# A hybrid decoder block on one core: transposed x as a second input, values of the first head group from raw x, the norm's row factor applied afterwards, and the first keys ahead of the first queries

## The chip, the cores and the metric

The kernel runs on one core of one Trainium2 chip. The metric is the device time of one execution in microseconds (us). A core has five engines that run side by side and meet at semaphores: TensorE (PE in the profile; its weight loads are PEld), VectorE (DVE), ScalarE (ACT), GpSimd (POOL) and SyncE (SP), which issues most of the DMAs. Each engine works through its own queue in the order in which the program stands.

## The reference

One sequence of 512 tokens of 1024 channels gets 16 meta tokens in front. The block normalises each row, multiplies it by one wide matrix and splits the result in eight parts; only the first four matter here:

```python
def rmsnorm(x, w):
    xf = x.astype(jnp.float32)
    y = xf * lax.rsqrt(jnp.mean(xf * xf, axis=-1, keepdims=True) + NORM_EPS)
    return (y * w.astype(jnp.float32)).astype(x.dtype)
...
u = rmsnorm(h, mix_norm_w[l])
proj = u @ w_in[l]
q, k, v, g_ret, lru_in, lru_gate, gate_a, gate_b = jnp.split(proj, split_at, axis=-1)
q = rotary(q.reshape(B, T, RET_HEADS, RET_QK_DIM).astype(f32), pos)
k = rotary(k.reshape(B, T, RET_HEADS, RET_QK_DIM).astype(f32), pos) * (RET_QK_DIM ** -0.5)
v = v.reshape(B, T, RET_HEADS, RET_V_DIM).astype(f32)
o = chunk_retention(q, k, v)
```

Behind it come a gated linear recurrence, gates that merge the two branches, an output projection and a feed-forward block with a second and a third rmsnorm. All is float32.

The norm has two factors: one per channel (the weight w) and one per row (the reciprocal root of the mean square). For a value row v = (x * w * r) @ W the row factor r can be applied to x before the product or to the finished row after it.

## The kernel before, in words

**Numbers.** A float32 operand is split into two parts, hi (a cast to the type that TensorE reads at full speed) and lo (the rest), and a product is made of three: hi by hi, hi by lo, lo by hi. So each quarter of a weight (128x512, called raw_...) costs one cast on ScalarE (line 290) and one subtraction on VectorE (line 294), and some go through POOL.

**Layout of x.** The 512 rows are four tiles of 128 tokens. TensorE needs the normed x with channels on the partitions. Before, x is loaded by rows (x_sb). For each tile ScalarE takes the sum of squares (Square with a sum, line 484), POOL makes the row factor and multiplies the identity by it (lines 476 to 490: a diagonal), and TensorE multiplies x by that diagonal (line 523, the uT tiles), which transposes and scales in one step; `halve` does half a tile, four blocks of 128 channels. Then `store` multiplies by the channel weight (line 508), casts (511) and subtracts (513). The result lies in four blocks, b11 and b21 (the lower and upper 512 channels of tokens 0 to 255), b12 and b22 (the same of tokens 256 to 511). Eight meta columns stand behind each of them, so a block is 264 columns wide, and 4 x 264 = 1056 in all.

**Fast and plain slabs.** A weight slab of 256 columns is either plain (four quarters; `plain512`, and for the keys 528 columns, `plain`) or fast: seven products instead of eight, with weight sums s1 to s4 on POOL (line 260) and four differences of x blocks, t1 to t4 (`sums_of`, lines 532 to 536: a subtraction, a cast and a subtraction each, on VectorE and ScalarE). The first queries Q0 are fast; the first keys K0, the first gates G0 and the values of the first head group are plain.

**The first stage.** The order of the first 45 us is written by hand in `FIRST_STEPS`: F is a row factor, T a transposition, x, h, l are the three steps of `store`, H and L the cast and the subtraction of the next weight quarter (P: the subtraction on POOL), W warm products, v the next step of `plain_values`. `plain_values` takes the eight quarters w_v for tile 0, tile 1, then both with the second four, then tiles 2 and 3; its accumulators are evicted by ScalarE (line 753). The meta rows get a path of their own (`norm_meta`, lines 567 to 585). Inside `manual_schedule` the engines keep the written order; behind it a planner orders each engine's queue. Then `ret_project` makes Q0, K0, G0, then the same for the other heads. Work that can be late (`defer`, `tick`) is put between products as their estimated time passes; `sums_of` for x is such an item, and in the first group it runs beside the last value products.

**Loads.** `FIRST_LOADS` is the order of the first DMAs on SyncE's queue: w0 to w3 are weight quarters of the values, x1 to x3 tiles, m the meta rows. Weight quarters have eight buffers (RAW), their hi and lo parts nine (RING).

Of the kernel before, what the change touches and what calls it, by code (L numbers as in the profile page):

```python
# [153 lines left out]
def hybrid_block(ctx: ExitStack, tc: tile.TileContext, a: dict):  # L154
# [16 lines left out]
    x_sb = [get(D) for t in range(NC_)]  # L171
    m_sb = get(D)
    nc.sync.dma_start(x_sb[0], a["x"][:C, :])
# [368 lines left out]
    UF, U, UFV, UV = blocks_of(TH)  # L542
    for load in FIRST_LOADS.split():
        if load[0] == "w":
            key, i, c = pieces[int(load[1:])]
            quarter(key, i, {"a11": 2, "a12": 3}[c])
        elif load == "m":
            nc.sync.dma_start(m_sb[:NM], a["meta"])
        else:
            t = int(load[1:])  # L550
            nc.sync.dma_start(x_sb[t], a["x"][t * C:(t + 1) * C, :])

    diags, halves = {}, {}

    def halve(t, c):

        pb = transposed(x_sb[t], diags[t], c, f"uT{t}_{c}")
        o = (t % 2) * C
        halves[t, c] = store(UFV, UV, pb, c, t // 2, slice(o, o + C), vec[:, V_MIX + 4 * c:V_MIX + 4 * c + 4])
        if c == 0:  # L560
            put(x_sb[t], diags.pop(t))
# [5 lines left out]
    def norm_meta():  # L567
        xn = get(D)
        nc.scalar.activation(xn[:NM], m_sb[:NM], AF.Copy, scale=diags.pop("m"))
        pm = bank("pm")  # L570
        for k in range(KT):
            nc.tensor.transpose(pm[:, k * NM:(k + 1) * NM], xn[:NM, k * P:(k + 1) * P], ident[:NM, :NM])
# [5 lines left out]
        nc.vector.tensor_tensor(um[:, :KT], pm, w, op=ALU.mult)
# [139 lines left out]
    def plain_values():  # L718

        acc = {}  # L720
        ws = {}
# [24 lines left out]
        pm = bank("vm0")
        for n, name in enumerate(PLAIN_V):
            _, h, c = name
            half, k = int(c[1]) - 1, int(c[2]) - 1
            value_meta(pm[:, half * 256:half * 256 + 256], ws[name], 4 * k + 2 * h, n == 0)  # L750
        vt = [get(D) for tok in range(2)]
        for t in range(NC_):
            nc.scalar.copy(vt[t // 2][:, t % 2 * 512:(t % 2 + 1) * 512], acc[t])
        vm = small.tile([2 * NM, 512], F32, tag="vm", bufs=2, name="vm0")
        nc.scalar.copy(vm, pm[:2 * NM])
# [4 lines left out]
    def first_steps(v):  # L760
        lows, meta = [], norm_meta()
        for step in FIRST_STEPS:
# [6 lines left out]
            elif kind in "LP":  # L769
                lows.pop(0)(nc.vector if kind == "L" else nc.gpsimd)  # L770
            elif kind == "W":
                keep_warm(WARM_MORE)
            elif step == "Fm":
                diags["m"] = rms_factors(m_sb[:NM], "m", NM, False)
            elif step in ("Tm", "xm"):
                next(meta, None)
            elif kind == "F":
                diags[int(t)] = rms_factors(x_sb[int(t)], f"x{t}")
            elif kind == "T":
                halve(int(t), int(c))  # L780
            elif kind in "xhl":
                next(halves[int(t), int(c)], None)
# [555 lines left out]
```

## Time and profile before

Three runs took 932.54, 933.21 and 933.74 us; the median is 933.21. The profile is one execution; its own time beyond the span isn't recorded, so its span of 930.1 us, from the first to the last instruction, stands for it.

| what | us |
|---|---|
| median of three runs | 933.21 |
| span of the profiled execution | 930.1 |
| first value product on TensorE | 12.81 |
| last meta product of the values | 45.34 |
| first product of Q0 | 45.46 |
| last product of K0 ends, Q0 already done | 67.4 |

A row of a timeline gives start, length, engine, line, operation, tiles (result <- operands, buffer numbers left out), shapes, count, and in brackets how long the engine stood idle before it and what released it. Rows of waits give the waiting engine and line, the one waited for, then total us, times and the longest. [...]

### The profile page before, as it was taken

What the parts mean: (1) busy time and instruction counts of PE and PEld (TensorE: products, weight loads), DVE (VectorE), ACT (ScalarE), POOL (GpSimd) and SP (SyncE); (2) the same over time, 40 slices, a digit from 0 to 9 for tenths busy, and PEclk for the clock granted to TensorE, in tenths of its full rate; (3) what the DMA queues carried; (4) which work ended last, traced back from release to release, by engine and by line L of the source; (5) the groups of instructions that cost most, each with busy time, mean ns of one, the idle gap of its engine ahead of it and who ended that gap; (6) DMA issues with size and microseconds to landing.
All of it is one profiled execution on the core that took longest, in us unless ns stands there. A gap on an engine that the chain in (4) does not pass through costs nothing.

```text
span 930.1 us, 16987 instructions
## 1 busy us (share of the span) xinstructions
PE 916.5 (99%) x6610; PEld 861.5 (93%) x6610; DVE 660.0 (71%) x905; ACT 460.7 (50%) x812; POOL 334.7 (36%) x243
## 2 busy tenths in 40 slices
PE   8999999999999999999999999999999999999996
PEld 7999999999999889999998888999999999888885
DVE  5877976996788837778745427868999999842223
ACT  6653544654455336847833325545555556632213
POOL 5234644454450001112200214458787785000003
PEclk9999999999999999999999999999999999999999
DMA  7142132231233332233442222223233323433202
GB/s 280 45 136 85 56 99 72 67 116 58 69 103 114 103 102 90 73 112 103 136 136 92 91 80 91 78 91 106 91 99 124 99 91 123 139 119 97 79 1 91
DMA packets 48496, 91.49 MB, mean 98 GB/s; under 512 B 5520, under 2 KB 5648, under 8 KB 48416
## 3 DMA queue, kind: packets, MB, share of 16 engines
q1 hardware_dynamic: 46976, 86.70, 28.8%
q10 hardware_dynamic: 1440, 3.71, 1.2%
q8 instruction: 52, 0.85, 0.4%
q14 instruction: 28, 0.23, 0.1%
HBM read 88.29 MB, written 2.10 MB: 97 GB/s over the span
## 4 chain that ended last, share of the span: by engine, by line
PE 93%; DVE 3%; DMA 1%; issue 1%; ACT 0%; SPq 0%; POOLq 0%; POOL 0%; DVEq 0%
PE fo L364 4%; PE fo L362 4%; PE fo L363 4%; PE zwf L372 4%; PE zwf L373 4%; PE zwf L374 4%; PE yxf L374 3%; PE yxf L373 3%; PE yxf L372 3%; PE lg L374 2%; PE gate L374 2%; DVE lo L294 2%; PE gate L372 2%; PE lg L372 2%; PE lg L373 2%; PE gate L373 2%
## 5 line engine op out<-in xcount | busy, mean ns | idle before, releaser
L294 DVE TENSOR_TENSOR lo<-raw_w_in,hi 128x512 fp32r<-128x512 f32 x99 | 81.7, 833 | 32.6 <-ACT hi L290 32.4
L290 ACT CAST hi<-raw_w_in 128x512 fp32r<-128x512 f32 x99 | 61.0, 622 | 61.5 <-PE w_br L363 13.9
L372 PE MATMUL zwf<-b,hi 128*128 128x256 f32 x304 | 85.7, 283 | 0.6 <-DVE pzf L393 0.6
L373 PE MATMUL zwf<-b,hi 128*128 128x256 f32 x304 | 85.0, 280 | 0.0
L294 DVE TENSOR_TENSOR lo<-s_w_fi,hi 128x512 fp32r<-128x512 f32 x76 | 76.1, 1028 | 12.6 <-ACT hi L290 8.8
L374 PE MATMUL zwf<-b,lo 128*128 128x256 f32 x304 | 85.0, 280 | 0.0
L294 DVE TENSOR_TENSOR lo<-raw_w_fo,hi 128x512 fp32r<-128x512 f32 x44 | 30.2, 691 | 61.9 <-ACT hi L290 61.9
L364 PE MATMUL fo<-hi,b 128*128 128x512 f32 x176 | 69.5, 395 | 0.0
L362 PE MATMUL fo<-hi,b 128*128 128x512 f32 x176 | 69.1, 394 | 0.0
L363 PE MATMUL fo<-lo,b 128*128 128x512 f32 x176 | 69.1, 392 | 0.0
L260 POOL TENSOR_TENSOR s_w_fi<-raw_w_fi,raw_w_fi 128x512 f32<-128x512 f32 x38 | 64.1, 1704 | 6.2 <-DVE lo L294 4.4
L294 DVE TENSOR_TENSOR lo<-raw_w_fi,hi 128x512 fp32r<-128x512 f32 x47 | 64.4, 1397 | 1.0 <-ACT hi L290 0.8
L374 PE MATMUL yxf<-b,lo 128*128 128x256 f32 x228 | 63.3, 281 | 0.0
L373 PE MATMUL yxf<-b,hi 128*128 128x256 f32 x228 | 63.3, 280 | 0.0
L372 PE MATMUL yxf<-b,hi 128*128 128x256 f32 x228 | 62.2, 280 | 0.2 <-ACT pzf L394 0.2
L290 ACT CAST hi<-raw_w_fo 128x512 fp32r<-128x512 f32 x44 | 27.3, 622 | 68.7 <-PE fo L364 63.7
L294 DVE TENSOR_TENSOR lo<-s_w_in,hi 128x512 fp32r<-128x512 f32 x52 | 49.1, 944 | 17.1 <-ACT hi L290 16.0
L372 PEld LDWEIGHTS zwf<-b,hi 128*128 128x128 f32 x304 | 56.9, 188 | 2.3 <-DVE pzf L393 2.3
L290 ACT CAST hi<-s_w_fi 128x512 fp32r<-128x512 f32 x76 | 45.9, 619 | 26.1 <-PE zwf L373 14.3
L290 ACT CAST hi<-raw_w_fi 128x512 fp32r<-128x512 f32 x69 | 42.0, 621 | 32.3 <-PE yxf L373 16.2
L373 PEld LDWEIGHTS zwf<-b,hi 128*128 128x128 f32 x304 | 57.3, 188 | 0.0
L374 PEld LDWEIGHTS zwf<-b,lo 128*128 128x128 f32 x304 | 57.3, 189 | 0.0
(412 smaller groups left out, 3301.4 us busy)
## 6 DMA issues: line engine op xcount, KB each, us to landing
raw_w_in<-in_w_in SPq DMA_DIRECT2D x112, 256.0 KB, 3.1
raw_w_fi<-in_w_fi SPq DMA_DIRECT2D x88, 256.0 KB, 3.4
raw_w_fo<-in_w_fo SPq DMA_DIRECT2D x44, 256.0 KB, 2.9
raw_w_v<-in_w_v SPq DMA_DIRECT2D x16, 256.0 KB, 4.5
raw_w_br<-in_w_br SPq DMA_DIRECT2D x16, 256.0 KB, 3.1
raw_w_bl<-in_w_bl SPq DMA_DIRECT2D x16, 256.0 KB, 3.3
raw_w_out<-in_w_out SPq DMA_DIRECT2D x16, 256.0 KB, 2.9
b<-in_x SPq DMA_DIRECT2D x4, 512.0 KB, 6.8
```

The costliest lines, as they stand in the source:

```text
L260: behind(nc.gpsimd.tensor_tensor(sums[key, i, name], x, y, op=op), state.get("diag"))
L290: nc.scalar.copy(hi, src)
L294: engine.tensor_tensor(lo, src, hi.bitcast(F32), op=ALU.subtract)
L362: nc.tensor.matmul(out, wh, xh, start=start, stop=False, skip_group_check=True)
L363: nc.tensor.matmul(out, wh, xl, start=False, stop=False, skip_group_check=True)
L364: nc.tensor.matmul(out, wl, xh, start=False, stop=stop, skip_group_check=True)
L372: nc.tensor.matmul(out, wh, xh, start=start and i == 0, stop=False, skip_group_check=True)
L373: nc.tensor.matmul(out, wh, xl, start=False, stop=False, skip_group_check=True)
L374: nc.tensor.matmul(out, wl, xh, start=False, stop=i == 3, skip_group_check=True)
```

## The change

- x is given to the kernel a second time, transposed on the host into the layout that TensorE needs (`xt`, one 128x1024 array for each tile), and the meta rows too (`mt`). The rows of x are still loaded, for the sums of squares alone.
- The transposed tile is multiplied by the channel weight in place (`weighted`, step f), then split into hi and lo without the row factor (`raw_high`, `raw_low`, steps h and l). The values are made from these raw parts, and the row factor is applied by ScalarE as the scale of the eviction (`evict`).
- For queries, keys, gates and the rest the normed blocks are still needed. `row_factor` (step q) makes the factor and its diagonal, `across` (step b) multiplies a matrix of ones by that diagonal on TensorE, which puts the 128 row factors of a tile side by side on every partition in one PSUM bank (rb), and `scaled` (step n) multiplies the weighted tile by it on VectorE; steps g and j cast and subtract as before.
- The meta products (`value_meta`) stand between the value products of tile 3 instead of behind all.
- K0 stands ahead of Q0 in the weights' order and in `ret_project`, and `sums_of` is finished behind K0's products instead of before the queries.
- The first loads are ordered anew, and the first weight quarter is issued from ScalarE's queue.

The diff, cut to its core (lines of the changed kernel are up to 74 higher):

```diff
+FIRST_STEPS = ("f01 h01 H l01 L f00 H h00 L l00 H L H L v f11 h11 f10 h10 l11 l10 v H L H L H L H L v "
+               "f21 h21 f20 h20 l21 l20 v f31 h31 f30 h30 qm q0 q1 l31 l30 v bm um b0 b1 "
+               "n00 g00 n01 g01 j00 j01 n10 g10 n11 g11 j10 j11 q2 q3 v "
+               "b2 b3 n20 g20 n21 g21 j20 j21 n30 g30 n31 g31 j30 j31").split()
...
-FIRST_LOADS = "w0 x1 w1 m w2 w3 x2 x3"
+FIRST_LOADS = "w1 w2 w3 x1 w4 w5 w6 w7 x2 m r0 r1 x3 r2 r3"
...
-            order += [("w_v", s)] * (s % 2 == 0) + [("w_in", Q + s), ("w_in", K + s), ("w_in", G + s)]
+            order += [("w_v", s)] * (s % 2 == 0) + [("w_in", b + s) for b in ((K, Q, G) if s == 0 else (Q, K, G))]
...
+    quarter(*pieces[0][:2], 3, nc.scalar)
+    nc.sync.dma_start(xt[0][:, :Q4], a["xt"][0][:, :Q4])
...
+    def weighted(t, c):
+
+        f = xt[t][:, half_tile(t, c)].rearrange("p (k t) -> p k t", k=4)
+        w = vec[:, V_MIX + 4 * c:V_MIX + 4 * c + 4].unsqueeze(2).broadcast_to([P, 4, C])
+        nc.vector.tensor_tensor(f, f, w, op=ALU.mult)
+
+    def raw_high(t, c):
+
+        if t not in raw:
+            raw[t] = get(D, F32R), get(D, F32R)
+        nc.scalar.copy(raw[t][0][:, half_tile(t, c)], xt[t][:, half_tile(t, c)])
+
+    def raw_low(t, c):
+
+        hi, lo = (p[:, half_tile(t, c)] for p in raw[t])
+        nc.vector.tensor_tensor(lo, xt[t][:, half_tile(t, c)], hi.bitcast(F32), op=ALU.subtract)
+
+    def row_factor(t):
+
+        i, n = (NC_, NM) if t == "m" else (t, P)
+        ssq = small.tile([P, 1], F32, tag="ssq", bufs=4, name=f"ssq_x{t}")
+        nc.scalar.activation(rows[t][:n], rows[t][:n], AF.Square, accum_out=ssq[:n])
...
+        nc.gpsimd.tensor_scalar(v[:n, :1], ssq[:n], 1.0 / D, EPS, ALU.mult, ALU.add)
+        nc.gpsimd.tensor_tensor(rx[:n, i:i + 1], v[:n, :1], mhalf[:n, :1], op=ALU.pow)
+        diags[t] = get(P)
+        state["diag"] = nc.gpsimd.tensor_scalar_mul(diags[t][:n, :n], ident[:n, :n], rx[:n, i:i + 1])
+
+    def across(t):
...
+        nc.tensor.matmul(out, ones[:n], d[:n, :n], start=True, stop=True)
...
+    def scaled(t, c):
...
+        r = cross["bank"][:, t * C:(t + 1) * C].unsqueeze(1).broadcast_to([P, 4, C])
+        nc.vector.tensor_tensor(f, xt[t][:, half_tile(t, c)].rearrange("p (k t) -> p k t", k=4), r, op=ALU.mult)
...
+        def evict(*tiles):
+            for t in tiles:
+                nc.scalar.activation(vt[t // 2][:, t % 2 * 512:(t % 2 + 1) * 512], acc[t], AF.Copy, scale=rx[:, t:t + 1])
+
+        for names, tiles in ((first, (0,)), (first, (1,)), (last, (0, 1)), (first, (2,)), (last, (2,)), (first, (3,)), (last, (3,))):
+            if names == last and tiles == (3,):
+                evict(0, 1, 2)
...
-            item = defer(sums_of(UF, U, UV, TH), 0.0)
+            list(v)
+            sums = defer(sums_of(UF, U, UV, TH), 0.0)
             tick(0)
-            list(v)
-            finish(item)
...
+        if s == 0:
+            finish(sums)
+            q = queries(s)
```

Where the instructions come to stand is shown at three places, with before's rows first. Tiles carry the number of this build. On **TensorE**, behind the values, before the change (vm0 are the meta rows, zwq0 is Q0):

```order
L666 MATMUL vm0_581<-hi7_322,us_134 32x256
L666 MATMUL vm0_581<-lo7_323,us_134 32x256
L372 MATMUL zwq0_628<-b26_468,hi8_488 128x256
L373 MATMUL zwq0_628<-b27_469,hi8_488 128x256
L374 MATMUL zwq0_628<-b26_468,lo8_489 128x256
```

and in the change, where K0's first half (k0_00) ends; rb is the bank of row factors, b13 the high part of b12, that is of tiles 2 and 3:

```order
L375 MATMUL k0_00_610<-b12_118,hi9_463 128x264
L376 MATMUL k0_00_610<-b11_117,lo9_464 128x264
L610 MATMUL rb_397<-b35_436,ones_79 128x128
L374 MATMUL k0_01_611<-b13_119,hi8_446 128x264
L374 MATMUL k0_10_612<-b9_115,hi10_479 128x264
L375 MATMUL k0_10_612<-b10_116,hi10_479 128x264
```

Behind the meta products stand now the third diagonal's product, 24 products of K0 on tokens 0 to 255, the fourth diagonal's, and then one product on tokens 256 to 511 ahead of the next group on tokens 0 to 255.

On **VectorE**, before the change, from the end of the meta part on (the rows of 1056 are `sums_of`):

```order
L583 COPY b9_113<-um_447 128x4x8
L422 TENSOR_TENSOR b17_121<-um_447,b16_120 128x4x8
L532 TENSOR_TENSOR b6_110<-b8_112,b6_110 128x1056
L532 TENSOR_TENSOR b8_112<-b9_113,b8_112 128x1056
L536 TENSOR_TENSOR b27_469<-b6_110,b26_468 128x1056
```

and in the change, around tiles 2 and 3 (b3_74 and b4_75 are these tiles weighted, lo11 to lo15 low parts of weights, b38 the rotated keys):

```order
L296 TENSOR_TENSOR lo11_496<-raw_w_in4_1_493,hi11_495 128x512
L296 TENSOR_TENSOR lo12_546<-s1_w_in0_533,hi12_545 128x512
L619 TENSOR_TENSOR b7_113<-b3_74,rb_397 128x4x128
L619 TENSOR_TENSOR b8_114<-b3_74,rb_397 128x4x128
L697 TENSOR_TENSOR b38_609<-k0_00_610,b22_159 128x264
L296 TENSOR_TENSOR lo13_560<-s3_w_in0_537,hi13_559 128x512
L296 TENSOR_TENSOR lo14_574<-raw_w_in0_3_541,hi14_573 128x512
L296 TENSOR_TENSOR lo15_588<-raw_w_in0_2_535,hi15_587 128x512
L846 TENSOR_TENSOR b14_120<-b7_113,b13_119 128x4x128
L846 TENSOR_TENSOR b16_122<-b8_114,b15_121 128x4x128
L619 TENSOR_TENSOR b7_113<-b4_75,rb_397 128x4x128
L619 TENSOR_TENSOR b8_114<-b4_75,rb_397 128x4x128
```

The factor of tile 3 (b4_75) stands behind the low parts of the first weights of Q0 and behind the rotation of K0's first half; `sums_of` follows after it.

On **ScalarE**, before the change, around the last Square (line 484, of the meta rows):

```order
L290 CAST hi6_306<-raw_w_v0_0_304 128x512
L290 CAST hi7_322<-raw_w_v1_0_320 128x512
L484 ACTIVATE b24_374,ssq_m_375<-b5_76 16x1024
L290 CAST hi8_488<-s1_w_in0_476 128x512
L511 CAST b16_120<-b9_113 128x4x128
```

and in the change, around the Squares of tiles 2 and 3 (line 594; b11 is the last cast of tile 1, hi8 to hi11 are K0's weights, hi12 Q0's first, line 805 the scaled evictions):

```order
L843 CAST b11_117<-b6_112 128x4x128
L594 ACTIVATE b20_151,ssq_x2_431<-b20_151 128x1024
L594 ACTIVATE b21_153,ssq_x3_438<-b21_153 128x1024
L292 CAST hi8_446<-raw_w_in4_2_444 128x512
L292 CAST hi9_463<-raw_w_in4_3_461 128x512
L292 CAST hi10_479<-raw_w_in4_0_477 128x512
L292 CAST hi11_495<-raw_w_in4_1_493 128x512
L805 ACTIVATE b26_189<-v2_320,rx_155 128x512
L816 COPY vm0_602<-vm0_187 32x512
L805 ACTIVATE b26_189<-v3_450,rx_155 128x512
L292 CAST hi12_545<-s1_w_in0_533 128x512
```

The Squares of tiles 2 and 3 come behind the casts of the normed tile 1, and K0's weights behind them.

More of the change, by code (lines that the diff above doesn't have):

```diff
@@ L170, in hybrid_block @@
     nc.scalar.dma_start(vec, a["vec"])
-    x_sb = [get(D) for t in range(NC_)]
-    m_sb = get(D)
-    nc.sync.dma_start(x_sb[0], a["x"][:C, :])
+    xt = [get(D) for t in range(NC_)]
+    nc.sync.dma_start(xt[0][:, Q4:], a["xt"][0][:, Q4:])
     mhalf = consts.tile([P, 4], F32, name="mhalf")
     nc.gpsimd.memset(mhalf, -0.5)
+    ones = consts.tile([P, P], F32, name="ones")
+    nc.gpsimd.memset(ones, 1.0)
     warm = consts.tile([P, 4], F32, name="warm")
@@ L249, in hybrid_block, with quarter @@
     sums = {}
-    def quarter(key, i, c):
+    def quarter(key, i, c, queue=None):
         if (key, i, c) not in raws:
             raws[key, i, c] = wpool.tile([P, Q4], F32, tag="raw", bufs=RAW, name=f"raw_{key}{i}_{c}")
-            nc.sync.dma_start(raws[key, i, c], a[key][i][:, c * Q4:(c + 1) * Q4])
+            (queue or nc.sync).dma_start(raws[key, i, c], a[key][i][:, c * Q4:(c + 1) * Q4])
         return raws[key, i, c]
@@ L542, in hybrid_block @@
     UF, U, UFV, UV = blocks_of(TH)
+    quarter(*pieces[0][:2], 3, nc.scalar)
+    nc.sync.dma_start(xt[0][:, :Q4], a["xt"][0][:, :Q4])
+    rows = {}
+    mt = consts.tile([P, KT, NM], F32, name="mt")
     for load in FIRST_LOADS.split():
+        t = int(load[1:] or 0)
         if load[0] == "w":
-            key, i, c = pieces[int(load[1:])]
-            quarter(key, i, {"a11": 2, "a12": 3}[c])
+            key, i, c = pieces[t]
+            quarter(key, i, {"a21": 0, "a22": 1, "a11": 2, "a12": 3}[c])
@@ L547, in hybrid_block @@
         elif load == "m":
-            nc.sync.dma_start(m_sb[:NM], a["meta"])
-        else:
[L550 to L561, printed above, removed]
+            rows["m"] = get(D)
@@ new lines, in hybrid_block, with half_tile @@
+            nc.sync.dma_start(rows["m"][:NM], a["meta"])
+            nc.sync.dma_start(mt, a["mt"].rearrange("p (k m) -> p k m", m=NM))
+        elif load[0] == "r":
+            rows[t] = get(D)
+            nc.sync.dma_start(rows[t], a["x"][t * C:(t + 1) * C, :])
+        else:
+            nc.sync.dma_start(xt[t], a["xt"][t])
+    rx = consts.tile([P, NC_ + 1], F32, name="rx")
+    raw = {}
+    diags = {}
+    cross = {}
+    def half_tile(t, c):
+        return slice(c * Q4, (c + 1) * Q4)
@@ L721, in plain_values @@
         ws = {}
+        meta = bank("vm0")
         def products(names, tiles):
@@ L760, in first_steps @@
     def first_steps(v):
-        lows, meta = [], norm_meta()
+        lows, parts = [], {}
         for step in FIRST_STEPS:
@@ L768, in first_steps, with queries @@
                 state["n"] += 1
[L769 to L782, printed above, removed]
+            elif kind == "L":
+                lows.pop(0)(nc.vector)
+            elif step == "um":
+                norm_meta()
+            elif kind == "q":
+                row_factor(t if t == "m" else int(t))
+            elif kind == "b":
+                across(t if t == "m" else int(t))
+            else:
+                t, c = int(t), int(c)
+                if kind == "n":
+                    parts[t, c] = scaled(t, c)
+                elif kind == "g":
+                    nc.scalar.copy(parts[t, c][1][0], parts[t, c][0])
+                elif kind == "j":
+                    f, (hi, lo) = parts.pop((t, c))
+                    nc.vector.tensor_tensor(lo, f, hi.bitcast(F32), op=ALU.subtract)
+                else:
+                    {"f": weighted, "h": raw_high, "l": raw_low}[kind](t, c)
+    def queries(s):
+        q = get(D)
+        q4 = q.rearrange("p (j n t) -> p j n t", j=2, n=2)
+        if plain_slab("w_in", Q + s):
+            rotate(q4, 256, [(j, slice(0, 2), pb) for j, pb in enumerate(plain512(Q + s, "q"))])
+        else:
+            fast512("w_in", Q + s, UV, q, "q")
+            rotate(q4, 256)
+        return q
     def ret_project(s):
```

64 lines of the change are left out of this document (32 added, 32 removed).

## The prediction

> **What bounds the kernel now.** I read the page's head first, then TensorE's waits, then busy time by stretch, then the timelines of the first 65 us engine by engine. Below stand the head's two lines, TensorE's waits over the whole run (total us, times, longest), and two stretches (bounds; length; busy us and counts of PE, PEld, DVE, ACT, POOL; granted clock; DMA share; GB/s).
>
> ```profile
> span 930.1 us, 16987 instructions
> PE 916.5 (99%) x6610; PEld 861.5 (93%) x6610; DVE 660.0 (71%) x905; ACT 460.7 (50%) x812; POOL 334.7 (36%) x243
> ...
> PE uT L523 <- POOL b L490: 2.4, 2, 1.2
> PE warm L185 <- POOL ident masks.py:199: 1.4, 1, 1.4
> PE v L363 <- DVE lo L294: 1.3, 2, 0.8
> PE o L895 <- DVE b L887: 0.8, 3, 0.3
> ...
> 12.80:45.60 32.80, 31.52 (x269) 30.71 (x268) 28.69 (x43) 20.20 (x38) 12.93 (x13) 1.00 0.31 113
> 45.60:67.40 21.80, 21.80 (x183) 21.80 (x182) 15.85 (x20) 12.95 (x26) 8.24 (x5) 1.00 0.46 146
> ```
>
> TensorE is the bound: it waits 1.4 us for the identity, 2.4 for diagonals, 1.3 for low weights, 0.8 late. In the stretches VectorE has 28.7 of 32.8 us filled while the values are made, and TensorE has no gap from 45.6 to 67.4, where it makes Q0 and K0. So a shift of the moment at which Q0 and K0 are both done passes to the end one for one. That moment, 67.4, is what I forecast anew. Its 180 products (84 for Q0, 96 for K0) take 21.8 us, **0.121 each**.
>
> **What the front of TensorE's queue gains.** Four rows of TensorE's timeline (start, length), two pieces of the chain of work that ended last, four rows of ScalarE's timeline, one of SyncE's, and from the DMA issues of the first 20 us the median time to landing:
>
> ```profile
> 1.38 4.78 PE L185 MATMUL warm<-ident 128*128 128x128 f32 x22 [1.38 <-POOL ident masks.py:199]
> 7.40 2.05 PE L523 MATMUL uT<-b,b 128*128 128x128 f32 x16 [1.23 <-POOL b L490]
> 9.29 0.60 PE L185 MATMUL warm<-ident 128*128 128x128 f32 x4
> 12.81 0.36 PE L362 MATMUL v<-hi,b 128*128 128x256 f32 x1
> ...
> 30.43 0.32 PE v L362
> 41.94 3.68 PE vm L666 x32
> ...
> 1.17 1.28 ACT L177 ACT_TABLE_LOAD   x1 [1.17 <-PEq L1328]
> 2.46 0.21 ACT L177 ACTIVATE warm<-mhalf 128x4 f32<-128x4 f32 x1
> 4.55 1.06 ACT L484 ACTIVATE b<-b 128x1024 f32<-128x1024 f32 x1 [1.88 <-DMA b<-in_x]
> 6.60 0.62 ACT L290 CAST hi<-raw_w_v 128x512 fp32r<-128x512 f32 x1 [0.89 <-DMA raw_w_v<-in_w_v]
> ...
> 0.72 0.38 SPq L173 DMA_DIRECT2D b<-in_x  x1
> ...
> raw_w_v<-in_w_v SPq DMA_DIRECT2D x8, 256.0 KB, 6.5
> ```
>
> Now the first value product waits for Square, factor, diagonal and the uT products; it starts at 12.81. After the change it waits for half a tile of transposed x (weighted on VectorE, cast on ScalarE) and for the first weight quarter, whose DMA stands on ScalarE's queue behind the table load and a small activation, thus at about 2.7. The first x took 0.72 to 4.55, 3.8 us; so that quarter lands near 6.5, its cast takes 0.62, and the first product runs at **7.4**. With the 6.5 us median flight of these quarters it would be 9.9, 2.5 later: an upper end.
>
> Products of the values: 96 of them from 30.43 to 41.94, 0.12 each, so all 192 take **23.0**; the meta rows 3.7. The uT groups go (2.05 each, four of them), and so do four warm products and the meta transposes; five products of ones by a diagonal come. The trace has none; a uT group of 16 records is 8 products, 0.26 each, so I take **1.1** for the five (nothing to 2, if they ran at a whole uT group).
>
> VectorE, ScalarE and POOL, rows of their timelines:
>
> ```profile
> 14.96 1.28 DVE L508 TENSOR_TENSOR b<-uT,vec 128x512 f32<-128x512 f32 x2
> 16.33 1.29 DVE L513 TENSOR_TENSOR b<-b,b 128x512 fp32r<-128x512 f32 x2
> 30.47 0.29 DVE L578 TENSOR_TENSOR um<-pm,vec 128x128 f32<-128x128 f32 x1 [1.50 <-PE pm L572]
> 32.47 2.55 DVE L532 TENSOR_TENSOR b<-b,b 128x1056 f32<-128x1056 f32 x2
> 67.71 0.42 DVE L642 TENSOR_TENSOR b<-k,b 128x264 f32<-128x264 f32 x1
> ...
> 16.80 1.05 ACT L484 ACTIVATE b<-b 128x1024 f32<-128x1024 f32 x1
> 17.86 1.12 ACT L290 CAST hi<-raw_w_v 128x512 fp32r<-128x512 f32 x2
> 36.33 0.59 ACT L753 COPY b<-v 128x512 f32<-128x512 f32 x1 [0.20 <-PE v L364]
> 46.62 0.57 ACT L755 COPY vm<-vm 32x512 f32<-32x512 f32 x1
> ...
> 5.79 0.19 POOL L476 TENSOR_SCALAR rv_x<-ssq_x 128x1 f32<-128x1 f32 x1 [4.46 <-ACT b L484]
> 6.73 0.61 POOL L490 TENSOR_SCALAR b<-ident,rr_x 128x128 f32<-128x128 f32 x1
> ```
>
> VectorE pays for it. A 128x512 subtraction or product costs it 0.64 (1.28 for two). Each half tile had two such (L508, L513) and now has four (weight, low part of raw, factor, low part of the normed); and the two low weight parts that POOL made go to VectorE: 18 more, 11.5 us. The earliest show at once: from 7.3, VectorE needs six steps to the fourth weight's low part and three more to tile 1, 9 x 0.64, until 13.0, where TensorE would be ready at 10.3 (24 products of 0.12 after 7.4). With small waits that is **3.0**. Then 7.4 + 23.0 + 3.7 + 0.6 (the first three new products) + 0.5 (the meta chain) + 3.0: values and meta end at **38.2**, 7.4 ahead of 45.6 (41.94 + 3.68). The value evictions now carry the row factor; ScalarE pays 0.59 as before.
>
> **What waits next.** K0's first half (24 products, 2.9) and the two late diagonals' products (0.5) follow; at **41.6** TensorE's queue has a product of K0's second half. It reads the high part of tiles 2 and 3, and every product behind it waits too. When is that part there? The steps, by the rows above:
> - The meta factor's product stands behind tile 2: 7.4 + 3.0 + 144 x 0.12 = 27.8. The meta chain to the end of its copies takes 2.0 (30.47 to 32.47), 30.1 with hand-overs. Factor and low part of tiles 0 and 1: 2.66 per tile (14.96 to 17.62), 35.5.
> - ScalarE has the Squares of tiles 2 and 3 behind tile 1's last cast (34.9): two at 1.06 (16.80 to 17.86), 37.1; then K0's first cast, 37.7. VectorE, with K0's low parts next in its queue, **idles 2.2**.
> - Low parts 8, 9, 10 by 39.7. The last diagonal is ready some 1.7 after its Square (the first one's ends at 5.61, its diagonal at 7.34), so POOL starts the four sums of Q0's weights near 39. Two such sums and two subtractions beside them:
>
> ```profile
> 54.98 1.75 POOL L260 TENSOR_TENSOR s_w_in<-s_w_in,raw_w_in 128x512 f32<-128x512 f32 x1
> 56.80 1.62 POOL L260 TENSOR_TENSOR s_w_in<-raw_w_in,s_w_in 128x512 f32<-128x512 f32 x1
> ...
> 56.09 1.18 DVE L294 TENSOR_TENSOR lo<-raw_w_in,hi 128x512 fp32r<-128x512 f32 x1 [0.52 <-ACT hi L290]
> 57.56 1.41 DVE L294 TENSOR_TENSOR lo<-s_w_in,hi 128x512 fp32r<-128x512 f32 x1 [0.29 <-ACT hi L290]
> ```
>
> - Beside such sums VectorE's subtraction takes 1.2 to 1.4 instead of 0.64, and four of them, at about 1.6, last to 45.4. Low part 11 so ends at 40.9. ScalarE makes four casts (0.56 each), three evictions (0.59, 0.57, 0.59) and cast 12 by 41.7: another 0.8 idle; low part 12 ends at 42.9.
> - Factors of tile 2, 1.3; K0's first rotation, 0.4; low parts 13 (beside POOL), 14, 15, 2.5; low parts of tile 2, 1.3; factor of tile 3, 0.7; its cast, 0.6: **49.7**.
>
> TensorE waits 49.7 - 41.6 = **8.1**; the 7.4 won are gone. [...]
>
> After it come 72 products of K0 (8.7) and a short wait for a low part (0.5): 58.9. Q0 follows, 10.1. Four sums and four low parts for it, 1.27 each (2.55 for two), stand on VectorE behind tile 3; K0 hides them but for what is left over: from 49.1, four steps of 0.64, 10.2 for the sums, three rotations of 0.42 and three low parts of 0.64 give 65.1 for the first low part of G0, plus 0 to 3 beside POOL's next sums; TensorE wants it at 64.9 (58.9, 48 products of Q0, two of G0). I take 1.2 there, and 0.7 and 1.2 for the next two hand-overs (Q0's middle sum, and scores of head 0), for VectorE stays behind: **3.1**, from 0 to 5. Total 58.9 + 10.1 + 3.1 = 72.1 against 67.4: **4.7 later**. The added DMAs (x comes twice, 4 MB instead of 2) cost nothing: the rows of x are read by the Squares alone, behind tile 3's casts at about 20, and transposed tiles 2 and 3 after the eight weight quarters are split, at 16; without that cover a tile is one flight late, 6.5. Against its own span the changed execution would have 930.1 + 4.7 = 934.8; the median shown, 933.21, lies 3.1 above the span, and with that it is **937.9**.
>
> **Rivals.**
> - *Sharing costs nothing, and VectorE has no backlog.* Low parts 11, 12, 13 take 0.64: 1.6 less, and the 3.1 go: 937.9 - 4.7 = 933.2. For it: VectorE's 71%. Against: the rows at 56.09 and 57.56. Chance 0.13.
> - *Faster: tiles 2 and 3 aren't late.* Were the Squares covered as well and ScalarE ahead of VectorE, the idle 2.2 and 0.8 would go too: 930.2. Its place is the wait for K0's second half; below 8.1 - 4.7 = 3.4 us there (that part ready before 45.0) the change gains. For it: ScalarE is busy 50%. Against: the Squares' place in its queue. Chance 0.11.
> - *The clock falls in the long wait.* No wait of TensorE in this trace is over 1.4 us after the start, so none shows it; but the first 22 warm products took 4.78, 0.22 each, against 0.13 per record in the uT row (2.05 for 16). If TensorE came back at half speed for as long, 2.4 more: 940.3. Backlog of VectorE would hide part of it. Chance 0.20. [...]
>
> **How the numbers follow.** The forecast has 0.56, its own range 935 to 940 (waits of 0 to 5, first product up to 2.5 later). 8 in 10 takes in the even case and the clock: 932.8 to 941.0. About 0.2% (1.9 us) is what a measurement can tell: faster 0.13 (its rival and 0.02 of the even case), same 0.13 (0.09 of the even case, 0.04 at the forecast's lower end), slower the rest, 0.74.
>
> **What would show it.** First value product near 7.4; meta products done near 38; a wait of some 8 us in front of K0's second half on the cast of tile 3; low parts near 1.2 us beside POOL's sums; three waits of about 1 us on VectorE from 64 to 90; nothing new later. It is wrong if that one wait is under 3.4, or if the first product comes after 9.

## The result, and the profile after

The changed kernel is slower: a median of 940.68 us (940.07 to 941.47, four runs) beside 933.15 for the kernel before, a ratio of 1.0083 with a 95% interval of 1.0071 to 1.0095. The profiled execution took 941.23 us, its span is 939.1, 9.0 longer than before's. The forecast was 937.9 in a range of 932.8 to 941.0.

The head of the changed kernel's page:

```profile
span 939.1 us, 16888 instructions
PE 914.2 (97%) x6544; PEld 858.3 (91%) x6544; DVE 673.0 (72%) x924; ACT 463.5 (49%) x819; POOL 331.6 (35%) x243
```

The two stretches that were shown of before, 12.8 to 45.6 and 45.6 to 67.4 us, in the changed kernel:

```profile
12.80:45.60 32.80, 27.20 (x233) 26.46 (x232) 22.10 (x44) 22.51 (x45) 13.27 (x19) 0.96 0.57 208
45.60:67.40 21.80, 17.92 (x129) 17.71 (x130) 21.80 (x24) 12.57 (x22) 6.68 (x4) 0.83 0.15 49
```

TensorE is busy for 2.3 us less in all than before (916.5) and has 66 products less (one behind the long wait fills 0.22 us, one before it 0.12), so the loss is waiting and slow products. It was full from 45.6 to 67.4; now it has 17.9 of these 21.8 us, at a granted clock of 0.83, and VectorE is the engine without a gap (21.80 of 21.80, before 15.85). TensorE's waits say what it stood for:

```profile
PE k L374 <- ACT b L843: 8.5, 1, 8.5
PE zwq L374 <- DVE pzq L395: 2.1, 1, 2.1
...
PE o L969 <- DVE b L961: 1.4, 3, 1.0
PE s L948 <- POOL b L703: 1.3, 1, 1.3
PE g L376 <- DVE lo L296: 0.9, 1, 0.9
```

TensorE's timeline gives the moments (L364 is a value product, L721 a meta product, L610 the ones product of tile 3, k is K0, zwq is Q0):

```profile
6.81 0.39 PE L364 MATMUL v<-hi,b 128*128 128x256 f32 x1 [0.83 <-ACT hi L292]
...
36.42 0.28 PE L721 MATMUL vm<-lo,us 128*32 128x256 f32 x1
...
39.68 0.38 PE L610 MATMUL rb<-b,ones 128*128 128x128 f32 x2
48.59 0.81 PE L374 MATMUL k<-b,hi 128*128 128x264 f32 x2 [8.52 <-ACT b L843]
49.19 0.42 PE L375 MATMUL k<-b,hi 128*128 128x264 f32 x1
49.41 0.42 PE L376 MATMUL k<-b,lo 128*128 128x264 f32 x1
...
53.27 0.28 PE L375 MATMUL k<-b,hi 128*128 128x264 f32 x1
...
72.38 0.39 PE L374 MATMUL zwq<-b,hi 128*128 128x256 f32 x1 [2.08 <-DVE pzq L395]
...
74.35 0.41 PE L375 MATMUL zwq<-b,hi 128*128 128x256 f32 x1
74.56 0.41 PE L376 MATMUL zwq<-b,lo 128*128 128x256 f32 x1
```

In these rows a length is more than the distance to the next start (0.28 beside 0.113 for the products around 36.42), so the pace is read from the starts. Products of hi and lo parts, 128x256, start 0.113 us apart there; before the change a float32 product of 128x128 took 0.26 (2.05 for the 8 of a uT group).

The values are done at 36.5 instead of 45.46: the front gained 8.9 us in this trace (in five other traces with the same steps up to there, the last meta product starts at 36.9 to 37.5 instead of 36.42). Then everything is given back. TensorE stands 8.5 us before K0's second half; behind that wait the products follow each other at 0.22 us (49.19, 49.41) until 53.1 and only then at 0.12, so 4.5 us of work are done at half speed (the granted clock is 0.50 from 42.88 to 53.12), some 2.0 lost. The same happens behind the 2.1 us wait in Q0, from 73.6 to 77.1 (74.35, 74.56: 0.21 apart): 1.6 lost. The later waits are 0.9, 2.1, 1.3 and, on the outputs, 0.6 more than before: 4.9. So -8.9 + 8.5 + 2.0 + 1.6 + 4.9 and 0.4 for the two late ones products make 8.5 of the trace's 9.0. By 119.5 us of before the loss is complete (the same product there starts at 128.9, 9.4 later; one near the end, at 796.4, is 9.1 later).

Why tile 3 was late stands on ScalarE, VectorE and POOL. Of the changed kernel (L594 Square, L619 factor product, L846 low part of the normed tile, L843 its cast, L296 low part of a weight, L395 Q0's middle sum, L262 sums of Q0's, later Q1's, weights):

```profile
34.16 1.05 ACT L594 ACTIVATE b<-b 128x1024 f32<-128x1024 f32 x1
47.91 1.22 ACT L843 CAST b<-b 128x512 fp32r<-128x512 f32 x2 [2.94 <-DVE b L619]
...
35.84 2.50 DVE L296 TENSOR_TENSOR lo<-raw_w_in,hi 128x512 fp32r<-128x512 f32 x4 [1.91 <-ACT hi L292]
40.75 1.09 DVE L296 TENSOR_TENSOR lo<-s_w_in,hi 128x512 fp32r<-128x512 f32 x1 [2.41 <-ACT hi L292]
43.30 1.57 DVE L296 TENSOR_TENSOR lo<-s_w_in,hi 128x512 fp32r<-128x512 f32 x1
47.21 1.27 DVE L619 TENSOR_TENSOR b<-b,rb 128x512 f32<-128x512 f32 x2
51.26 3.47 DVE L846 TENSOR_TENSOR b<-b,b 128x512 fp32r<-128x512 f32 x2
...
71.91 0.41 DVE L395 TENSOR_TENSOR pzq<-zwq,wsq 128x256 f32<-128x256 f32 x1
...
41.26 1.72 POOL L262 TENSOR_TENSOR s_w_in<-s_w_in,raw_w_in 128x512 f32<-128x512 f32 x1
43.05 1.27 POOL L262 TENSOR_TENSOR s_w_in<-raw_w_in,s_w_in 128x512 f32<-128x512 f32 x1
48.79 3.69 POOL L262 TENSOR_TENSOR s_w_in<-raw_w_in,raw_w_in 128x512 f32<-128x512 f32 x2 [4.46 <-DMA raw_w_in<-in_w_in]
```

The Squares of tiles 2 and 3 end at 35.2, VectorE idles 1.9 and 2.4 us for casts that stand behind them and behind POOL's sums, and beside these sums a low part takes 1.09 and 1.57 instead of 0.64. That is the chain which the forecast had written down. VectorE's busy time from 41 to 73 us, of the kernel before and then of the changed one, shows what follows it:

```profile
41.00:73.00 32.00, 23.75 (x31) 1.00 0.36 116
```

The changed kernel:

```profile
41.00:73.00 32.00, 32.00 (x35) 0.84 0.21 70
```

VectorE had 8.25 us to spare there and has none now.

### The profile page after: what moved, and what is told of

It reads as the page before. It is cut to its first block, busy times and chain, and to the rows that moved or that the text cites. A ratio compares the mean times of both kernels' runs of the same rounds, so it can differ in the third digit from the quotient of the medians.

```text
span 939.1 us, 16888 instructions
## 1 busy us (share of the span) xinstructions
PE 914.2 (97%) x6544; PEld 858.3 (91%) x6544; DVE 673.0 (72%) x924; ACT 463.5 (49%) x819; POOL 331.6 (35%) x243
## 4 chain that ended last, share of the span: by engine, by line
PE 87%; DVE 3%; issue 1%; POOL 0%; ACT 0%; POOLq 0%; DVEq 0%
PE fo L366 4%; PE fo L365 4%; PE fo L364 4%; PE zwf L374 4%; PE zwf L375 4%; PE zwf L376 4%; PE yxf L376 3%; PE yxf L375 3%; PE yxf L374 3%; DVE lo L296 2%; PE lg L374 2%; PE gate L374 2%; PE gate L376 2%; PE lg L376 2%; PE gate L375 2%; PE lg L375 2%
## 5 line engine op out<-in xcount | busy, mean ns | idle before, releaser
L296 DVE TENSOR_TENSOR lo<-raw_w_in,hi 128x512 fp32r<-128x512 f32 x99 | 81.9, 837 | 30.8 <-ACT hi L292 28.6
L296 DVE TENSOR_TENSOR lo<-s_w_fi,hi 128x512 fp32r<-128x512 f32 x76 | 74.8, 1012 | 14.3 <-ACT hi L292 10.3
L296 DVE TENSOR_TENSOR lo<-raw_w_fo,hi 128x512 fp32r<-128x512 f32 x44 | 30.2, 690 | 61.9 <-ACT hi L292 61.9
L364 PE MATMUL fo<-hi,b 128*128 128x512 f32 x176 | 69.1, 393 | 0.0
L262 POOL TENSOR_TENSOR s_w_fi<-raw_w_fi,raw_w_fi 128x512 f32<-128x512 f32 x38 | 64.1, 1706 | 6.2 <-DVE lo L296 4.9
L296 DVE TENSOR_TENSOR lo<-raw_w_fi,hi 128x512 fp32r<-128x512 f32 x47 | 64.2, 1392 | 1.1 <-ACT hi L292 0.9
L296 DVE TENSOR_TENSOR lo<-s_w_in,hi 128x512 fp32r<-128x512 f32 x52 | 50.3, 970 | 18.0 <-ACT hi L292 17.0
```

The costliest lines, as they stand in the source:

```text
L262: behind(nc.gpsimd.tensor_tensor(sums[key, i, name], x, y, op=op), state.get("diag"))
L296: engine.tensor_tensor(lo, src, hi.bitcast(F32), op=ALU.subtract)
L364: nc.tensor.matmul(out, wh, xh, start=start, stop=False, skip_group_check=True)
```

## Experiments

Two questions were open: how much of the loss is the one wait for tile 3 ("late tiles"), the clock, or VectorE's backlog as a whole; and what, if anything, keeps the 8.9 us. All edits are to the changed kernel unless said; line numbers shift by a few between the kernels. Ratios are against runs of the kernel before made beside each kernel; 0.001 is 0.93 us. Beside squares_early, warm_fill, queries_first and keys_first_alone those runs spread from 931.8 to 934.7 us, so gains are taken from the ratios, and two ratios less than some 0.0015 apart are not told apart.

**Squares of tiles 2 and 3 earlier.**

```diff
-"... f31 h31 f30 h30 qm q0 q1 l31 l30 v bm um b0 b1 n00 ... j11 q2 q3 v b2 b3 ..."
+"... f31 h31 f30 h30 qm q0 q1 q2 q3 l31 l30 v bm um b0 b1 n00 ... j11 v b2 b3 ..."
```

> One move in the order of the first steps: the Squares of tiles 2 and 3 stand right behind that of tile 1, no longer behind tile 1's casts. Theory 'late tiles' (TensorE's 8.5 us wait is set by the chain Squares - diagonals - VectorE's factors and low parts - ScalarE's cast of tile 3, which holds VectorE idle for some 1.9 + 2.4 us on the way): VectorE fills those gaps, the wait falls by 3 to 4 us to about 5, and the kernel's time with it, to 936.5 to 938. Rival 'backlog' (VectorE simply has too much to do by 80 us; the wait only shows where): the wait shrinks, but the microseconds come back as waits of the Q0, G0 and score products on VectorE, and the time stays above 939.5. Theory 'clock' (part of the loss is the granted clock, which stood at 0.50 for 4.5 us behind the wait): with a wait of about 5 us the clock still falls, so nothing more than the wait is won.

937.83 us, 1.0051 [1.0038, 1.0065], 3.0 us better. Its waits:

```profile
PE k L374 <- ACT b L843: 5.5, 1, 5.5
PE zwq L374 <- DVE pzq L395: 2.5, 1, 2.5
```

The wait fell by 3.0 and the time by as much: the Squares' place is worth 3 of the 8.5 us, and at this size the backlog did not take it back.

**The wait filled with work.**

```diff
-"b2 b3 n20 g20 ..."
+"b2 b3 k n20 g20 ..."
...
+            elif kind == "k":
+                keep_warm(40)
```

> 40 products of the identity with itself, at 0.20 us each 8 us, are issued on TensorE right behind the ones products of tiles 2 and 3, so that TensorE works through the wait for tile 3's cast. Nothing else moves. Theory 'clock': the granted clock stays at 1.00 where it was 0.50, the first 20 products of K0's second half take 0.12 us apiece and not 0.22, 2.0 us are won, and with the second slow stretch (73.7 to 77 us) up to 3.5: 937.2 to 938.7. Rival 'backlog': what TensorE wins there it loses in its next waits on VectorE, 940 to 941. If the fill ends later than tile 3's cast, each product too many costs 0.2 us.

939.95 us, 1.0075 [1.0061, 1.0089]: not told apart from the changed kernel. The fill was too short. Two rows of TensorE's timeline:

```profile
40.79 4.53 PE L187 MATMUL warm<-ident 128*128 128x128 f32 x40
49.50 0.81 PE L374 MATMUL k<-b,hi 128*128 128x264 f32 x2 [4.18 <-ACT b L845]
```

And the stretch 48 to 54 (the clock stands third from the end):

```profile
48.00:54.00 6.00, 4.50 (x20) 4.50 (x21) 6.00 (x7) 2.29 (x3) 4.14 (x3) 0.50 0.22 73
```

At a granted clock of 1.00 the 40 products take 4.5 us, not the 8 that the slow ones at the start had suggested; a wait of 4.2 was left, and behind it the clock stood at 0.50. So it was done again with `keep_warm(76)`:

> As warm_fill, where the 40 products took 0.11 us apiece at the full clock and so only 4.3 of the 8.5 us, and the clock still fell to 0.50 in the 4.2 us that were left. Now 76 of them, 8.1 us, so that at most a short wait stays. Theory 'clock': K0's second half runs at 1.00 throughout; against the changed kernel 2.0 us are won there, and up to 1.5 more at 73.7 to 77 us if the clock stays up there too: 937 to 939. Rival 'backlog': the products wait for VectorE later instead, by as much, and the time stays at 940 to 941.

940.78 us, 1.0086 [1.0073, 1.0100]: nothing won. The same stretch:

```profile
48.00:54.00 6.00, 4.54 (x37) 4.09 (x35) 6.00 (x7) 2.29 (x3) 3.84 (x3) 1.00 0.20 64
```

Two of TensorE's waits:

```profile
PE zwq L374 <- DVE pzq L395: 3.2, 2, 2.6
...
PE k L375 <- DVE b L848: 1.2, 1, 1.2
```

And rows of VectorE's timeline: tile 3's factor, the low part that the new wait is for, and Q0's middle sum:

```profile
48.07 1.27 DVE L619 TENSOR_TENSOR b<-b,rb 128x512 f32<-128x512 f32 x2
52.13 3.45 DVE L848 TENSOR_TENSOR b<-b,b 128x512 fp32r<-128x512 f32 x2
...
72.75 0.41 DVE L395 TENSOR_TENSOR pzq<-zwq,wsq 128x256 f32<-128x256 f32 x1
```

The clock stayed at 1.00 and K0's second half ran at 0.12 us a product (49.79, 49.91), into a new wait of 1.2 us for tile 3's low part (beside POOL 3.45 for two instead of 1.28) and a longer one for Q0's middle sum (3.2 against 2.1). In this trace everything up to tile 3 is 0.8 us later than in the changed kernel's (K0's first product starts at 37.51 instead of 36.67, ahead of the fill), but VectorE's way from tile 3's factor to Q0's middle sum takes the same 24.7 us (48.07 to 72.75, and 47.21 to 71.91), and TensorE's from the start of K0's second half to the product that waits for that sum 23.8 in both. So at K0 the slow clock had cost nothing of its own up to there: while TensorE crept, VectorE caught up. In the time itself the runs would not show a gain under some 1.4 us.

**Queries first again, and keys first alone.** The first undoes one part of the change:

```diff
-order += [("w_v", s)] * (s % 2 == 0) + [("w_in", b + s) for b in ((K, Q, G) if s == 0 else (Q, K, G))]
+order += [("w_v", s)] * (s % 2 == 0) + [("w_in", b + s) for b in (Q, K, G)]
...
+        if s == 0:
+            finish(sums)
+        q = queries(s)
```

> The rest of the change, but Q0 stays ahead of K0 as it was before. Q0 needs all four sums of tile blocks, whose last low part ends at 65.8 us in the changed kernel, and no K0 products stand in front of it to cover. Theory 'late tiles': TensorE, done with the value products at 36.5 us, waits some 15 us for the sums, and the time is 944 to 948. Rival 'the new order of keys and queries is what costs': the time falls back towards 933 to 936.

The second makes that part alone in the kernel before:

```diff
-order += [("w_v", s)] * (s % 2 == 0) + [("w_in", Q + s), ("w_in", K + s), ("w_in", G + s)]
+order += [("w_v", s)] * (s % 2 == 0) + [("w_in", b + s) for b in ((K, Q, G) if s == 0 else (Q, K, G))]
...
-            finish(item)
...
+        if s == 0:
+            finish(sums)
+            q = queries(s)
```

> The kernel before with only the order of K0 and Q0 exchanged. There TensorE arrives at both with every operand ready (0.0 to 0.5 us of waits), so each theory expects no change, 932.7 to 933.7. If the exchange itself costs (rotation of the keys, the later Q0 casts), it shows here: above 935.

Queries first: 943.34 us, 1.0109 [1.0095, 1.0122], just under the range that "late tiles" gave, and far from its rival. Its one long wait:

```profile
PE zwq L374 <- ACT b L537: 15.3, 1, 15.3
```

Keys first alone: 933.33 us, 0.9996 [0.9987, 1.0005], no change. So the exchange of keys and queries is harmless by itself and covers some 2.4 us (1.0109 - 1.0083) where the tiles are late.

**Q0 in the plain form.**

```diff
-PLAIN_R = "K0 G0 K1 K3 G3".split()
+PLAIN_R = "Q0 K0 G0 K1 K3 G3".split()
```

> Q0's eight quarter products in the plain form (four weight quarters, no sums on GpSimd), the rest as in the changed kernel. It takes away the sums of Q0's weights that GpSimd makes at 38.8 to 44.3 us and three low parts on VectorE, and adds 12 products on TensorE, 1.4 us. Theory 'sharing' (VectorE's instructions beside GpSimd's sums take up to 1.6 us instead of 0.68 and hold tile 3's cast back): the wait falls from 8.5 to about 7, the waits on Q0's sums (2.1 us) go, and the time falls by 1.5 to 3.5 us, to 937 to 939. Rival 'late tiles alone' (sharing is covered): the wait stays at 8 to 8.5 and the 12 added products show, 941 to 942.5.

932.11 us, 0.9993 [0.9984, 1.0002]: 8.4 us better than the changed kernel, more than twice the best that was expected. Its longest wait:

```profile
PE k L374 <- ACT b L843: 5.6, 1, 5.6
```

And VectorE's row for the two low parts that stand ahead of tile 2's:

```profile
42.07 1.28 DVE L296 TENSOR_TENSOR lo<-raw_w_in,hi 128x512 fp32r<-128x512 f32 x2
```

The wait lost 2.9 us, and the waits of Q0, G0 and the scores are gone altogether. To part GpSimd's sums from the rest, they were put back with nobody reading them:

```diff
+        if (key, i, c) == ("w_in", Q, "a11"):
+            s1 = combine(key, i, "s1", a21(), a22(), ALU.add)
+            combine(key, i, "s3", a11(), a21(), ALU.subtract)
+            s2 = combine(key, i, "s2", s1, a11(), ALU.subtract)
+            combine(key, i, "s4", a12(), s2, ALU.subtract)
```

> As q0_plain, but GpSimd makes Q0's four sums at their old place all the same; nothing reads them. What differs from q0_plain is GpSimd's work alone, what differs from the changed kernel is VectorE's three low parts, ScalarE's three casts and TensorE's 12 products. Theory 'sharing' (q0_plain won because GpSimd no longer lengthens VectorE's instructions at 38.8 to 44.3 us): tile 3's cast comes 1 to 2 us later again and the time rises from 932.1 by 1.5 to 4 us, to 933.5 to 936. Rival 'less to do' (it won because VectorE has three low parts less and Q0 no longer hangs on sums that come late): it stays at 932 to 933.

934.91 us, 1.0024 [1.0015, 1.0033]. Its longest wait:

```profile
PE k L379 <- ACT b L848: 8.7, 1, 8.7
```

VectorE's rows at the same place (factor products, then the two low parts), and POOL's beside them:

```profile
41.76 1.27 DVE L624 TENSOR_TENSOR b<-b,rb 128x512 f32<-128x512 f32 x2
42.95 3.46 DVE L301 TENSOR_TENSOR lo<-raw_w_in,hi 128x512 fp32r<-128x512 f32 x2
...
39.84 3.13 POOL L262 TENSOR_TENSOR s_w_in<-raw_w_in,raw_w_in 128x512 f32<-128x512 f32 x2
42.94 1.26 POOL L262 TENSOR_TENSOR s_w_in<-s_w_in,raw_w_in 128x512 f32<-128x512 f32 x1
44.27 1.59 POOL L262 TENSOR_TENSOR s_w_in<-raw_w_in,s_w_in 128x512 f32<-128x512 f32 x1
```

Two low parts take 3.46 beside the sums and 1.28 without them (and the seven ahead of them 5.47 instead of 4.40); the wait is back at 8.7, and 2.9 us of time (0.0031) go with GpSimd's work alone. The other 5.5 (1.0083 - 1.0024) come from what hung on VectorE behind: three low parts less, and no Q0 product that waits for a sum of blocks. By the traces, waits of 0.9, 2.1, 1.3 and 1.2 (outputs) and the 1.6 of slow clock in Q0 are gone, and 1.4 of added products come, 5.7 in all. Not tried apart: which of the two reliefs counts more.

The control, the same line in the kernel before:

> The kernel before with Q0 in the plain form, nothing else: a control. Theory 'backlog' (the plain form pays only where VectorE is behind): in the kernel before VectorE has 8 us to spare between 41 and 73 us, so the 12 added products show, 1.4 us more, 934 to 934.8 beside 933.2. Rival 'the plain form of Q0 is better by itself': below 932.5.

931.14 us, 0.9983 [0.9974, 0.9991]. This expectation was wrong, the rival right: the plain form is better there too, by 1.6 us. The stretch 13 to 36 us in the kernel before and in this one (busy us of PE, PEld, DVE, ACT, POOL):

```profile
13.00:36.00 23.00, 21.72 (x184) 21.15 (x183) 19.97 (x33) 13.52 (x27) 12.73 (x13) 1.00 0.44 156
```

With Q0 plain:

```profile
13.00:36.00 23.00, 22.49 (x193) 22.13 (x192) 18.63 (x35) 13.99 (x26) 5.39 (x9) 1.00 0.42 154
```

Q0's sums on POOL (12.7 us there, now 5.4) had stood beside VectorE's low parts of the values, and TensorE gets 0.8 us more into this stretch. Q0 starts at 44.17 instead of 45.46; that pays for the 12 products (G0 starts at 67.4, before 67.2), and up to 113 us the two kernels are level. The gain itself, 1.1 us in the traces, comes at output products between 113 and 118 us, where 0.5 us of waits on VectorE are gone; the rest of it is not explained. The plain form gives 1.6 before and 8.4 after the change; by that difference, 6.8 is what the sums and low parts cost where VectorE is late.

**Row factors earlier.** The Squares and diagonals are pulled to where VectorE idles, and the ones products of tiles 2 and 3 go to a bank of their own.

```diff
-"... f21 h21 f20 h20 l21 l20 v f31 h31 f30 h30 qm q0 q1 l31 l30 v bm um b0 b1 n00 ... j11 q2 q3 v b2 b3 n20 ..."
+"... f21 h21 f20 h20 qm q0 l21 l20 v q1 f31 h31 f30 h30 q2 q3 l31 l30 bm um b0 v b1 n00 ... j11 b2 b3 v n20 ..."
...
+    def row(t):
+
+        return cross["bank"][:, t * C:(t + 1) * C] if t < 2 else pw[:, t * C:(t + 1) * C]
```

> The row factors are brought forward in the order of the first steps: the Squares of meta and tile 0 stand behind tile 2's casts, those of tiles 1 to 3 beside tile 3's, the ones products of tiles 2 and 3 stand ahead of the last value products, and write to a bank of their own, so that they need not wait until VectorE has read those of tiles 0 and 1. Theory 'late tiles': VectorE's idle stretches of 5.1, 1.9 and 2.4 us fill, tile 3's cast comes 5 to 6 us earlier, the wait shrinks to 2.5 to 3.5 us, the clock falls little or not at all, and the time is 930.5 to 934, near the kernel before or under it. Rival 'backlog' (VectorE's added 16 instructions per stage, about 10 us, are the floor whatever their order): the wait only moves to the Q0, G0 and score products, and the time stays above 936.

934.76 us, 1.0021 [1.0012, 1.0030], a little above its range. Its first waits:

```profile
PE k L371 <- ACT b L844: 3.7, 1, 3.7
PE zwq L371 <- DVE pzq L392: 2.2, 2, 1.5
```

Then the same with steps and loads interleaved further (of the steps the diff shows the end):

```diff
-"... b1 n00 g00 n01 g01 j00 j01 n10 g10 n11 g11 j10 j11 b2 b3 v n20 g20 n21 g21 j20 j21 n30 ..."
+"... b1 bm b0 um n00 g00 n01 n10 g10 g01 j00 n11 v v g11 j10 j11 b2 n20 g20 n21 b3 g21 j20 j21 j01 n30 ..."
...
-FIRST_LOADS = "w1 w2 w3 x1 w4 w5 w6 w7 x2 m r0 r1 x3 r2 r3"
+FIRST_LOADS = "w3 w1 w2 x1 w5 m w6 x2 w4 r0 w7 x3 r1 r3 r2"
```

> As rows_early, with the first loads and steps interleaved further by a search over their order, every instruction the same: row factors of the meta rows before tile 2's weights, b2 and b3 behind the last value products, loads of the rows in between those of the weights. Theory 'late tiles': the waits ahead of K0 shrink to two of 0.5 to 1.3 us, the clock stays at 1.00, and nearly all of the 8.9 us that the front is ahead stays, less the waits of the early value products: 927 to 931, under both kernels. Rival 'backlog': not under 933.

931.72 us, 0.9987 [0.9979, 0.9996], above its range too, but under the kernel before. Its first waits:

```profile
PE zwq L371 <- DVE pzq L392: 2.8, 2, 1.6
PE k L372 <- DVE b L847: 2.3, 1, 2.3
```

The wait at K0 shrinks to 3.7 and 2.3, and the one in Q0 stays at 2.2 and 2.8. Order (with that bank) wins 5.8 and 9.0 us, the second more than the whole loss of 7.7, so the lateness was mostly one of order; what is left are waits on VectorE.

**Both together.** The edits of rows_early and q0_plain in one kernel.

> rows_early and q0_plain together. Theory 'backlog' (what counts is when VectorE has caught up): the two reliefs add in part. q0_plain still waits 5.6 us at K0 and has no later wait; rows_early still waits 3.7 us at K0 and some 4 us later on. Together a wait of about 2 us at K0 and nothing behind it: against q0_plain 3 to 4 us less, 928 to 929.5, under both kernels. Rival 'the same microseconds counted twice': 931 to 932.

928.09 us, 0.9953 [0.9940, 0.9965]: within the range, and 4.4 us under the kernel before. Its wait at K0:

```profile
PE k L371 <- ACT b L844: 1.5, 1, 1.5
```

And VectorE from 36 to 67 us:

```profile
36.00:67.00 31.00, 31.00 (x38) 1.00 0.36 113
```

Steps and loads were interleaved once more, with Q0 plain:

```diff
-FIRST_LOADS = "w1 w2 w3 x1 w4 w5 w6 w7 x2 m r0 r1 x3 r2 r3"
+FIRST_LOADS = "w1 w3 w2 w4 x1 x2 w5 w6 r0 w7 m r3 x3 r1 r2"
...
-"... qm q0 l21 l20 v q1 f31 h31 f30 h30 q2 q3 l31 l30 bm um b0 v b1 n00 ..."
+"... qm L L f20 L h21 h20 q0 v l21 f31 q3 f30 h30 v l20 h31 v q1 b0 bm v um b1 v l31 q2 n00 ..."
```

> As rows_early_q0_plain with the first loads and steps interleaved by a search over their order; every instruction is the same. What order can still win there are the waits that are left in rows_early_q0_plain: 1.5 us at K0, 0.3 at zwq, 0.8 at the first outputs, 2.6 in all, and some of the early waits of the value products on casts and low parts (0.9). Theory 'backlog' (VectorE is full from 36 to 67 us in every one of these kernels, so what is won at K0 comes back behind it): at most 1 us, 927 to 928.5. Rival 'late tiles' (each microsecond of the wait at K0 counts): 2 to 3 us, 925 to 926.5.

928.52 us, 0.9959 [0.9946, 0.9973]: no better, as "backlog" had it. Its first wait at K0 is 1.7 us (on tile 3's low part), and VectorE is as full (30.90 of the 31 us). But a full VectorE does not show that order has nothing left to win: in rows_early it has no gap from 36 to 67 us either (31.00, 35 instructions), and rows_earliest, as full (31.00, 38 instructions), is 3.2 us faster by the order of steps and loads alone; instructions that stand beside POOL's sums fill time too. This order starts K0 1.1 us later (38.67 instead of 37.56), so what it may have won behind that it lost ahead of it. Beside the kernel before with Q0 plain (0.9983), the change so ordered is worth 0.30%, 2.8 us.

## Why the prediction came out as it did

The direction, the place and the mechanism were right; the size was 2.8 us short in the medians, 4.3 in spans (934.8 forecast, 939.1 seen). The measured 940.68 lies above the forecast's own range of 935 to 940. It lies within the wider one, up to 941.0, because that one took in the clock's 2.4 us, which cost nothing at K0; that part is luck. In spans the 4.3 are roughly -1.5 (front), 0.4 (the wait at K0), 3.6 (slow clock; the 2.0 at K0 stand where waits would have been) and 1.8 (later waits). By its steps:

- **First value product, 7.4.** It came at 6.81. The DMA of the first weight quarter was put behind ScalarE's table load, at 2.7; it was issued at 1.24. Values and meta ended at 36.5, 1.7 earlier than the 38.2 of the forecast: 0.6 by this start, and some 1.3 because from 13 us on the products followed each other at 0.113 us (36.31, 36.42), where the forecast took 0.12.
- **The wait at K0's second half, 8.1.** 8.5 was seen: TensorE was there at 40.1 instead of 41.6 and went on at 48.6 instead of 49.7. Its parts hold: the Squares' place (squares_early, 3.0), and GpSimd beside VectorE, priced at 1.6 in the first rival and worth 2.9 (q0_plain_sums_idle against q0_plain).
- **Later waits, 3.1, from 0 to 5.** This is the term that was mis-sized. Waits of 4.9 were seen, with 1.6 of slow clock between them; and with the clock held up behind K0 (warm_fill_long) the 2.0 us won there came back as waits. The backlog so is between 4.9, just inside the range, and 7 (4.9 + 2.0). The sum let VectorE's 16 us of work behind tile 3's cast (49.1 to 65.1) nearly hide behind K0, all at lengths without GpSimd but for "0 to 3" at its end; yet POOL's sums of Q1's weights fell beside tile 3's own low parts, 3.47 for two instead of 1.28 (the row at 51.26).
- **The clock rival, 2.4.** Its event came: 2.0 us at K0 and 1.6 in Q0. Its price, as an addition, was wrong at K0: taking the slow clock away there gave 940.78 for 940.68. In Q0 it seems to cost: warm_fill's clock stayed at 1.00 there, and from Q0's restart to the product that is at 119.5 before its trace takes 53.8 us (73.28 to 127.1) instead of 56.5 (72.38 to 128.9), of which 0.6 is a shorter wait of the scores. Its time, 939.95, is too near to tell, and this was not tried alone.
- **The even rival (933.2)** needed GpSimd to cost nothing and VectorE to have no backlog; both fell. **The faster one (930.2)** was to decide at a wait under 3.4 us: rows_early, with 3.7, is 0.2% slower than the kernel before, rows_earliest, with 2.3 and 0.2, is 0.1% faster. The point was well placed, though what lies behind the wait counts too.
- "Nothing new later" held.

## What to carry to other kernels

Work taken off the bounding engine's front is worth only as much as the engine that takes it over has to spare in the same stretch: add up that engine's instructions up to the moment where all must be ready, not its share of the whole span (VectorE stood at 72% of the span, and at 100% from 41 to 73 us). When such an engine is behind, first look for what can leave it or stand beside it (here 12 more products on TensorE took sums off GpSimd and low parts off VectorE, and the time fell by 8.4 us), then for order. A slow stretch of TensorE that sits in front of another engine's backlog can be real and yet cost nothing (here the 2.0 us at K0: 940.78 us without the slow clock there, 940.68 with it).

## What the runs showed of the hardware that was not expected

- **GpSimd's sums lengthened some of VectorE's instructions and not others.** In q0_plain_sums_idle the two low parts (both inputs in SBUF) took 3.46 instead of 1.28 beside GpSimd's sums, and the factor products just ahead of them, with one input in PSUM (rb) and also beside such sums, took their usual 1.27. That the place of the inputs makes the difference is not shown: no run moved them. It is not always VectorE that is held up: in q0_plain the first sum of blocks (at 46.17, both inputs in SBUF) took its usual 1.25 beside two sums of GpSimd that took 3.60, where one with VectorE idle (at 73.95) takes 1.30.
- **The clock fell after a short wait in one trace and not in another.** In stretches of 0.1 us, the granted clock of the changed kernel falls to 0.50 or comes back to 1.00 at 8.75, 12.16, 42.88, 53.12, 73.60 and 77.01 us. The steps between these are 1, 9, 3, 6 and 1 times 3.41 us; that it is set at the ends of stretches of this length is an estimate from these six moments. It falls at the end of three of them, and in these TensorE is busy for 59% (up to 8.75), 17% (up to 42.88; the 8.5 us wait began in it) and 39% (up to 73.60; it holds the 2.1 us wait in Q0). In warm_fill the clock falls at 48.02, and counted on from there in steps of 3.41 one ends at 71.9, in the middle of a wait of 2.3 us; TensorE is busy for 73% and 60% of those on both sides, and the clock stays at 1.00. How busy a stretch must be for the clock to stay is not shown.
- **Early on the record of the clock and the pace of the products can disagree.** From 8 to 13 us the record shows 0.66 in the changed kernel and 1.00 in rows_early_q0_plain and queries_first. In the changed kernel products of the values start 0.21 us apart from 9.12 to 11.99, where the record stands at 0.50; in rows_early_q0_plain they start as far apart (8.28, 8.50, 8.71), with the record at 1.00. In these 5 us TensorE has 26, 26 and 25 products in the three, and VectorE is busy for 4.83 in each; whether it sets the pace there was not tested.
